# Routed experts on one core: weights split into two fp32r parts or kept whole in fp32, a ring of 9 or 17 weight places, and small experts in two or four column groups

## The chip, the cores and the metric

The kernel runs on one core of one Trainium2 chip. The metric is the time of one execution on the device in microseconds; the median of several runs counts. All rows below come from one execution that the profiler recorded.

## The reference

One block of a hybrid encoder over 1024 tokens of width 1024, all in float32: a state-space mixer and stick-breaking attention, an output projection with a residual, and then a routed mixture of 32 experts, which is the part that the change is about.

```python
h2 = rms_norm(x, g_ffn)                       # g_ffn: one factor per column
gates, expert_id = router(h2)                 # 2 of 32 experts per token
for e in range(32):                           # rows of expert e, in blocks of 128
    y[rows] += gate * ((silu(xb @ w_gate[e]) * (xb @ w_up[e])) @ w_down[e])
x = x + y        # w_gate, w_up: [32, 1024, 512]; w_down: [32, 512, 1024]
```

Each expert has three matrices of 2 MB, 201 MB in all, and each is read once from HBM. With the inputs of the reference its routing gives the 32 experts these numbers of tokens: ten have 32 or fewer (11 to 31), twelve have 33 to 64, six have 65 to 128 (67 to 124), two have 129 to 192 (162, 177) and two have more (198, 219).

## The kernel before

**Stages.** The input projection, the mixer and the attention come first; then the output projection runs over 8 tiles of 128 tokens (`out_open`, `out_part`, `out_close`), with the norm, the store of the normed rows to the DRAM tensor `h2d` (`norm_store`) and the router (`router_turn`, `router_tile`) of each tile. Up to here the order is made by a scheduler. From `moe = tc.manual_schedule(...)` on PE, ACT, DVE and POOL run in the order of the code; only SP's queue, which issues the weight loads, is placed by the scheduler.

**The loop over experts.** Step `e` of the loop computes `in_(e)` (gate and up products), `in_out(e)` (SiLU and product), `prep_x(e + 1)` (the next expert's rows, turned by PE), `down_(e - 1)`, `h_(e)` (the hidden rows turned), and prepares later experts: `prep` makes a one-hot table on DVE, `prep_p` takes row numbers and gates from it on PE, `prep_f` and `prep_g` gather rows of `h2d` by indirect DMAs from POOL, and `down_` ends with an indirect DMA that adds rows to `out` (`scatter`). Experts 0 to 2 come in their own order; the other 29 are sorted by their counts and interleaved (`expert_order`), so that large ones stand among small ones: by counts the order begins 38, 39, 36, 29, 162, 35, 62, 22, 198, 41, 70, 27 and ends 35, 67, 27, 98, 29, 45, 11.

**Sizes.** Expert 0 is always treated as one of over 64 tokens. The count is read into registers of each engine, and branches (`tc.If`) choose the code:

- up to 64 tokens ("few"): the weights are used as they are, in fp32, as the moving operand. The array's 128 columns are two halves of 64: gate goes to PSUM partitions 0 to 63 and up to 64 to 127 (`in_mm_few`), and the two column halves of the down product likewise (`down_mm_few`). 16 matmuls of 512 columns in, 8 down.
- over 64: `w_split` makes of each half matrix a rounded fp32r part `wh` (ACT) and the rest `wl` (DVE), the rows are split too, and each product is three fp32r matmuls (`split_mm`): 48 in, 24 down for a block of 128 tokens. A second block has a second set (`gx`), or the "few" code if it has up to 64 tokens.

**The weight ring.** `units` lists the half matrices, 1 MB each, in the order of use: 4 for `in_`, 2 for `down_`, 192 in all. `load_units` issues them on SP's queue into ring places of 8 KB per partition. There are `RA + RB = 9` places: 5 that are there from the start, and 4 that are made once the tensors of the mixer are given up. A load waits until the unit 9 before it has been used. The first 16 units belong to experts 0 to 2; the later ones need the sorted order, which SP reads from `evi`. The out-projection's weights lie in the `wh` and `wl` buffers (`w_parts`, 8 of each).

Of the kernel before, what the change touches and what calls it, by code (L numbers as in the profile page):

```python
# [18 lines left out]
D = 1024  # L19
# [17 lines left out]
def block_kernel(ctx, tc, x, g_mix, w_in, lam_re, lam_im, log_dt, b_re, b_im, c_re, c_im, d_skip,  # L37
# [11 lines left out]
    mixs = ExitStack()  # L49
    mixp = mixs.enter_context(tc.tile_pool(name="mixp", bufs=1, side="left"))  # L50
# [713 lines left out]
    hlp = ctx.enter_context(tc.tile_pool(name="hlp", bufs=1, side="right", reuse_waits="tile"))  # L764
    HL = 8

    def w_parts():
        return [hlp.tile([P, D], FR, name=nm, bufs=HL) for nm in ("wh", "wl")]

    p3 = o3.enter_context(tc.tile_pool(name="p3", bufs=1, side="right", reuse_waits="tile"))  # L770
# [3 lines left out]
    wo = [w_parts() for _ in range(8)]  # L774
# [3 lines left out]
    gffn_b = p3.tile([P, D], F32, name="gffn_b")  # L778
    nc.scalar.dma_start(gffn_b, dram(g_ffn, 0, [[0, P], [1, D]]))
# [3 lines left out]
    gpc = p3.tile([P, 8], F32, name="gpc")  # L783
# [42 lines left out]
    RA, RB = 5, 4  # L826
    LK = RA + RB
# [7 lines left out]
    rings = {}  # L835
# [12 lines left out]
    def load_units(n):  # L848

        while loaded[0] < min(n, len(units)):  # L850
            k_ = loaded[0]
            ap, s_, rows, hf = units[k_]
            e = s_
            if s_ >= NF:
                if s_ not in ev_sp:
                    ev_sp[s_] = nc.values_load(evs[0][0:1, s_:s_ + 1], engines=[mybir.EngineType.SP],
                                               min_val=0, max_val=NE - 1)
                e = ev_sp[s_]
            pool, nb = (rga, RA) if k_ % LK < RA else (rings["b"], RB)
# [5 lines left out]
    load_units(RA)  # L865


# [39 lines left out]
    slotm = kp.tile([P, P], BF, name="slotm")  # L907
    ts(top, slot, 64.0, 64.0, op0=OP.is_ge, op1=OP.mult)
    tt(slotm, slot, top, op=OP.subtract)
    ts(slot2m, slotm, float(P), None, op0=OP.add)  # L910

    side = kp.tile([P, 1], F32, name="side")
    ts(side, pcol, 64.0, None, op0=OP.is_ge)

# [160 lines left out]
    for i in range(NT):  # L1075
# [11 lines left out]
        if i < NT - 1:  # L1087
            out_close(i)
        if i >= 2:
# [6 lines left out]
    many = kp.tile([P, NE], F32, name="many")  # L1096
    evi = kp.tile([P, NE], I32, name="evi")
    csi = kp.tile([P, NE], I32, name="csi")
    evs.append(evi)
    def expert_order():  # L1100
        tmp = mo.tile([P, 3, NE], F32, name="tmp", tag="gs")
# [11 lines left out]
        ts(many[:, NF:NE], kv, 65.0 * NE, None, op0=OP.is_ge)  # L1113
        ki = mo.tile([P, NS], I32, name="ki")
# [8 lines left out]
    EX = {0: {"in": [], "ins": [], "down": [], "downs": []}}  # L1123
    raw_k, used = [0], [0]

    def early_split(js, eng):
        for j in js:
            raw = raws.pop(raw_k[0])
            raw_k[0] += 1
            parts = [w_parts() for _ in range(2)]  # L1130
            EX[0]["in"].append(raw)
            EX[0]["ins"].append(parts)
            for q_ in range(2):
                r = raw[:, D * q_:D * q_ + D]
                nc.scalar.copy(parts[q_][0], r)
                eng.tensor_tensor(parts[q_][1], r, parts[q_][0].bitcast(F32), op=OP.subtract)
# [7 lines left out]
    early_split(range(1), nc.gpsimd)  # L1144
# [5 lines left out]
    gate_parts(0, NT - 1, nc.gpsimd, nc.scalar.copy)  # L1150
# [4 lines left out]
    tt(away, away, cnt.unsqueeze(1).to_broadcast(sh), op=OP.mult)  # L1155

    tt(posb, own, away, op=OP.add)
# [5 lines left out]
    one_hot(OH, posb[:, :, 0:1], slotb)  # L1163
# [8 lines left out]
    LO, HI, AL = slice(0, HP), slice(HP, P), slice(0, P)  # L1172
# [14 lines left out]
    def x_turn(xg, cg, pt):  # L1187
        for c in range(4):
            nc.tensor.transpose(pt[:, c], xg[:, 4 * cg + c::8], ident)

    def in_mm(blocks, hv):

        for hf in range(2):
            for pa, xh, xl in blocks:
                for k_ in range(4 * hf, 4 * hf + 4):
                    ws = slice(512 * (k_ % 2), 512 * (k_ % 2) + 512)
                    for j in range(2):
                        wh, wl = hv[2 * hf + j][k_ % 4 // 2]
                        split_mm(pa[j], xh[:, k_], xl[:, k_], wh[:, ws], wl[:, ws], k_ == 0, k_ == 7)

    def in_mm_few(pg, xt, hv):
        for k_ in range(8):
            for r, j in ((LO, 0), (HI, 1)):
                w = hv[2 * (k_ // 4) + j]
                mm(pg[r], xt[:, k_], w[:, 512 * (k_ % 4):512 * (k_ % 4) + 512],  # L1205
                   start=k_ == 0, stop=k_ == 7)

    def down_mm(blocks, hv):
        for c in range(4):
            wh, wl = hv[c // 2][c % 2]  # L1210
            for n in range(2):
                ns = slice(512 * n, 512 * n + 512)
                for py, hh, hl in blocks:
                    split_mm(py[n], hh[:, c], hl[:, c], wh[:, ns], wl[:, ns], c == 0, c == 3)

    def down_mm_few(py, ht, hv):
        for c in range(4):
            for n, r in enumerate((LO, HI)):
                w = hv[c // 2]
                mm(py[r], ht[:, c], w[:, D * (c % 2) + 512 * n:D * (c % 2) + 512 * n + 512],  # L1220
                   start=c == 0, stop=c == 3)

# [4 lines left out]
    def prep(e):  # L1227
# [7 lines left out]
        if e:  # L1235
            sl = kp.tile([P, P], BF, name="sl")
            stt(sl, top, many[:, e:e + 1], slotm, op0=OP.mult, op1=OP.add)
# [35 lines left out]
    def prep_it(e):  # L1273
# [9 lines left out]
        with nc.allow_low_precision(reason="whole numbers below 2048"):  # L1283
            nc.vector.tensor_reduce(idx[:, 0:n], d["pi"][:, 0:n, TOK], op=OP.add, axis=AX.X)
            ts(idx[:, 2:2 + n], idx[:, 0:n], 2.0, side, op0=OP.mult, op1=OP.add)
# [14 lines left out]
    def prep_f(e):  # L1300
# [9 lines left out]
        with many_.Else():  # L1310
            gather(d["xg"], d["idx"], LO)
# [20 lines left out]

    def prep_x(e):
# [4 lines left out]
        d["xf"] = xf = mo.tile([P, 8, HP], F32, name="xf", bufs=2)  # L1338
        d["xt"] = xt = mo.tile([P, 8, P], FR, name="xt")
        d["xl"], d["xh2"], d["xl2"] = (mo.tile([P, 8, P], FR, name=nm) for nm in ("xl", "xt2", "xl2"))  # L1340
        xl, xh2, xl2 = d["xl"], d["xh2"], d["xl2"]
        pts = [pb("tr").rearrange("p (c t) -> p c t", c=4) for _ in range(2)]
        pts2 = [pb("gx").rearrange("p (c t) -> p c t", c=4) for _ in range(2)]
        cs = [slice(4 * cg, 4 * cg + 4) for cg in range(2)]
        with tc.If(d["nt"] > P) as two:
            for cg in range(2):
                x_turn(d["xg"], cg, pts[cg])
            for cg in range(2):
                x_turn(xgb, cg, pts2[cg])
        with two.Else():  # L1350
            for cg in range(2):
                x_turn(d["xg"], cg, pts[cg])
        with tc.If(d["na"] > HP) as many_:
            for cg in range(2):
                nc.scalar.copy(xt[:, cs[cg]], pts[cg])
            with tc.If(d["na"] > P):
                with tc.If(d["na"] <= P + HP) as few:
                    nc.scalar.copy(xf[:, cs[0]], pts2[0][:, :, LO])
                with few.Else():
                    for cg in range(2):  # L1360
                        nc.scalar.copy(xh2[:, cs[cg]], pts2[cg])
        with many_.Else():
            nc.scalar.copy(xf[:, cs[0]], pts[0][:, :, LO])
        with tc.If(d["nv"] > HP) as many_:
# [348 lines left out]
```

## Time and profile before

| | |
|---|---|
| time, median of 3 runs | 1335.95 us (1335.26 to 1337.76) |
| the profiled execution: its own time | 1337.16 us |
| its span, first to last instruction | 1335.2 us |
| mean granted clock of TensorE in the span | 0.922 |
| matmul rows in the loop over experts | 606.06 us to 1323.2 us |

The span is what the rows below divide. The execution's own time is 2.0 us longer than its span, and 1.2 us longer than the median of the runs.

### The profile page before, as it was taken

What the parts mean: (1) busy time and instruction counts of PE and PEld (TensorE: products, weight loads), DVE (VectorE), ACT (ScalarE), POOL (GpSimd) and SP (SyncE); (2) the same over time, 40 slices, a digit from 0 to 9 for tenths busy, and PEclk for the clock granted to TensorE, in tenths of its full rate; (3) what the DMA queues carried; (4) which work ended last, traced back from release to release, by engine and by line L of the source; (5) the groups of instructions that cost most, each with busy time, mean ns of one, the idle gap of its engine ahead of it and who ended that gap; (6) DMA issues with size and microseconds to landing.
All of it is one profiled execution on the core that took longest, in us unless ns stands there. A gap on an engine that the chain in (4) does not pass through costs nothing. (4 is left out here: it accounts for less than half of the span.)

```text
span 1335.2 us, 21708 instructions
## 1 busy us (share of the span) xinstructions
PE 1132.6 (85%) x6986; PEld 809.8 (61%) x6986; DVE 773.1 (58%) x1510; ACT 490.3 (37%) x820; POOL 274.3 (21%) x408
## 2 busy tenths in 40 slices
PE   5999999979998899948778989887898688888885
PEld 5999999957766478835335455554456354445541
DVE  6888776797879567778343245553535541445420
ACT  6233534466775532224132133341323420333321
POOL 4141211043345112242111101111101111011101
PEclk9999999979999899977889989988898889889888
DMA  7242321110002343533897968899956989698895
GB/s 249 78 87 53 81 53 53 49 48 1 1 4 82 140 176 127 196 134 114 302 348 270 358 245 337 280 358 382 372 204 243 362 285 354 274 348 290 294 348 174
DMA packets 96744, 272.09 MB, mean 204 GB/s; under 512 B 44324, under 2 KB 57448, under 8 KB 71944
## 3 DMA queue, kind: packets, MB, share of 16 engines
q1 hardware_dynamic: 81528, 238.05, 48.6%
q0 software_dynamic: 12192, 29.93, 9.1%
q8 instruction: 129, 2.11, 0.6%
q10 hardware_dynamic: 2800, 1.22, 0.4%
q14 instruction: 95, 0.78, 0.2%
HBM read 242.56 MB, written 25.43 MB: 201 GB/s over the span
## 5 line engine op out<-in xcount | busy, mean ns | idle before, releaser
L1205 PE MATMUL acc<-raw,xf 128*64 128x512 f32 x672 | 155.4, 610 | 5.5 <-issue 5.5
L1395 DVE TENSOR_TENSOR wl<-raw,wh 128x1024 fp32r<-128x1024 f32 x124 | 143.8, 1219 | 21.6 <-ACT wh L1392 18.0
L92 PE MATMUL acc<-wh,hTh 128*128 128x256 f32 x512 | 146.4, 286 | 4.3 <-ACT wh L88 4.3
L93 PE MATMUL acc<-wl,hTh 128*128 128x256 f32 x512 | 145.1, 283 | 0.0
L94 PE MATMUL acc<-wh,hTl 128*128 128x256 f32 x512 | 144.4, 282 | 0.0
L1392 ACT CAST wh<-raw 128x1024 fp32r<-128x1024 f32 x124 | 121.4, 1048 | 30.2 <-DMA raw<-in_w_down_dram 18.3
L1205 PEld LDWEIGHTS acc<-raw,xf 128*64 128x64 f32 x672 | 51.7, 140 | 93.8 <-issue 90.6
L1429 ACT ACTIVATE hs<-acc 128x512 f32<-128x512 f32 x32 | 19.1, 596 | 231.3 <-PE acc L94 90.8
L1179 POOL DMA_INDIRECT xga<-h2d,idx x32 | 31.3, 978 | 342.0 <-PE y L1220 103.6
L92 PEld LDWEIGHTS acc<-wh,hTh 128*128 128x128 f32 x512 | 97.0, 190 | 4.9 <-ACT wh L88 4.9
L698 DVE TENSOR_TENSOR_SCAN bb<-bb,sb 128x128 f32<-128x128 f32 (+7 forms) x64 | 89.6, 1416 | 13.3 <-POOL bb L695 12.7
L93 PEld LDWEIGHTS acc<-wl,hTh 128*128 128x128 f32 x512 | 96.9, 189 | 0.7 <-DVE wl L89 0.6
L94 PEld LDWEIGHTS acc<-wh,hTl 128*128 128x128 f32 x512 | 96.8, 189 | 0.0
L92 PE MATMUL acc<-wh,xt 128*128 128x512 f32 x176 | 74.8, 425 | 13.7 <-ACT wh L1392 6.4
L695 POOL TENSOR_SCALAR bb<-sb 128x128 f32<-128x128 f32 (+7 forms) x64 | 66.2, 1038 | 94.0 <-ACT sb L694 82.7
L1220 PE MATMUL y<-raw,hf 128*64 128x512 f32 x336 | 82.1, 633 | 3.6 <-DVEq L1500 2.3
L94 PE MATMUL acc<-wh,xl 128*128 128x512 f32 x176 | 73.2, 416 | 0.4 <-DVE xl L1366 0.4
L93 PE MATMUL acc<-wl,xt 128*128 128x512 f32 x176 | 73.0, 415 | 0.0
L1184 POOL DMA_INDIRECT out_dram<-ysa,idx x23 | 38.0, 1653 | 115.3 <-ACTq L1390 37.6
L1433 DVE TENSOR_TENSOR hs<-hs,acc 128x512 f32<-128x512 f32 x11 | 7.6, 687 | 91.5 <-ACT hs L1429 61.4
L92 PE MATMUL y<-wh,ht 128*128 128x512 f32 x88 | 41.8, 475 | 20.9 <-PEq L1482 7.5
L1501 DVE TENSOR_SCALAR ysf<-y,gate 128x512 f32<-128x512 f32 x11 | 8.3, 751 | 83.3 <-PE y L94 65.4
(473 smaller groups left out, 2480.7 us busy)
## 6 DMA issues: line engine op xcount, KB each, us to landing
raw<-in_w_gate_dram SPq DMA_DIRECT2D x64, 1024.0 KB, 13.8
raw<-in_w_up_dram SPq DMA_DIRECT2D x64, 1024.0 KB
raw<-in_w_down_dram SPq DMA_DIRECT2D x64, 1024.0 KB, 14.3
wraw<-in_w_in_dram SPq DMA_DIRECT2D x16, 512.0 KB
wor<-in_w_out_dram SPq DMA_DIRECT2D x8, 512.0 KB, 4.9
xt<-in_x_dram SPq DMA_DIRECT2D x8, 512.0 KB, 7.5
out_dram<-xt SPq DMA_DIRECT2D x8, 512.0 KB, 2.9
h2d<-h SPq DMA_DIRECT2D x8, 512.0 KB, 3.5
```

The lines of the kernel that those rows point to most:

```text
L92: mm(o, ah, bh, start=first, stop=False)
L93: mm(o, ah, bl, start=False, stop=False)
L94: mm(o, al, bh, start=False, stop=last)
L695: nc.gpsimd.tensor_scalar(bt[:, off:T], st[:, off:T], -1.0, 1.0, op0=OP.mult, op1=OP.add)
L698: nc.vector.tensor_tensor_scan(rv, rv, sv, 0.0, op0=OP.mult, op1=OP.add)
L1179: nc.gpsimd.indirect_dma_start(out=dst[r], out_offset=None, in_=h2d, in_offset=bass.IndirectOffsetOnAxis(ap=idx[:n, :1], axis=0))
L1184: nc.gpsimd.indirect_dma_start(out=rows, out_offset=bass.IndirectOffsetOnAxis(ap=idx[:n, :1], axis=0), in_=src[r], in_offset=None, compute ...
L1205: mm(pg[r], xt[:, k_], w[:, 512 * (k_ % 4):512 * (k_ % 4) + 512], start=k_ == 0, stop=k_ == 7)
L1220: mm(py[r], ht[:, c], w[:, D * (c % 2) + 512 * n:D * (c % 2) + 512 * n + 512], start=c == 0, stop=c == 3)
L1392: nc.scalar.copy(w[0], r)
L1395: tt(w[1], r, w[0].bitcast(F32), op=OP.subtract)
L1429: act(hs, pg, AF.Silu)
```

## The change

- Weights are never split. All products with expert weights are fp32 matmuls on the ring places themselves (`in_all`, `in_half`, `in_quarter`, `down_all`, `down_half`, `down_quarter`); `w_split`, `early_split` and `w_parts` go, and with them the parts of the rows (`xl`, `hl`, ...).
- A third size: an expert of up to 32 tokens uses four column groups of 32. `in_quarter` puts gate and up of the first four and of the last four row groups on one group each, so that 4 rounds of 4 matmuls take the place of 8 rounds of 2; a matmul with a table `fold` adds the two partial sums while it turns them. `down_quarter` has 2 rounds of 4. Gathers take 32 rows, and scatters 64 half rows.
- The ring has 17 places: the 5 of before, two in `q_t` and two in `yT` (kept for the whole kernel now), and 8 (`rgw`) where the out-projection's weights lay. 16 units are issued when the out-projection ends, the 17th after `expert_order`.
- `g_ffn` no longer multiplies the stored rows (DVE, or POOL for the last tile); ACT stores them with the norm's factor alone, and DVE applies `g_ffn` when it copies the turned rows out of PSUM (`x_scaled`). The last tile's store goes on ACT's queue.
- In the steps ahead of the loop, the places and gates of all experts are worked out after expert 0's gather has been issued.

```diff
-    RA, RB = 5, 4
-    LK = RA + RB
+    ring = [rga.tile([P, 2048], F32, name=f"rg{j}") for j in range(5)]
+    ring += [q_t.rearrange("p t n -> p (t n)")[:, 2048 * j:2048 * j + 2048] for j in range(2)]
+    ring += [yT.rearrange("p k c t -> p (k c t)")[:, 2048 * j:2048 * j + 2048] for j in range(2)]
+    LK = len(ring) + 8
...
-            t_ = pool.tile([P, 2048], F32, name="raw", tag="raw", bufs=nb)
+            t_ = ring[k_ % LK]
             nc.sync.dma_start(t_.rearrange("p (c n) -> p c n", c=rows), wsrc(ap, e, hf, rows))
...
-        if i == NT - 1:
-            nc.gpsimd.tensor_tensor(h2, d["x2"], gffn_b, op=OP.mult)
-            act(h2, h2, AF.Copy, scale=d["r"])
-        else:
-            stt(h2, d["x2"], d["r"], gffn_b, op0=OP.mult, op1=OP.mult)
-        nc.sync.dma_start(h2d[i * P:(i + 1) * P, :], h2)
+        act(h2, d["x2"], AF.Copy, scale=d["r"])
+        (nc.scalar if i == NT - 1 else nc.sync).dma_start(h2d[i * P:(i + 1) * P, :], h2)
...
-    early_split(range(1), nc.gpsimd)
+    wo_s.close()
+    rgw = ctx.enter_context(tc.tile_pool(name="rgw", bufs=1, side="right", reuse_waits="tile"))
+    ring.extend(rgw.tile([P, 2048], F32, name=f"rw{j}") for j in range(8))
+    load_units(16)
...
+    def x_scaled(xt, cg, pt, r):
+        n = r.stop - r.start
+        cs = slice(4 * cg, 4 * cg + 4)
+        tt(xt[:, cs, r], pt[:, :, r], gpc[:, cs].unsqueeze(2).to_broadcast([P, 4, n]), op=OP.mult)
+
+    def in_all(p, xt, hv):
+        for k_ in range(8):
+            for j in range(2):
+                mm(p[j], xt[:, k_], hv[2 * (k_ // 4) + j][:, 512 * (k_ % 4):512 * (k_ % 4) + 512],
+                   start=k_ == 0, stop=k_ == 7)
...
+    def in_quarter(pg, xt, hv):
+        for k_ in range(4):
+            for u in range(4):
+                mm(pg[32 * u:32 * u + 32], xt[:, 4 * (u // 2) + k_, QU], hv[u][:, 512 * k_:512 * k_ + 512],
+                   start=k_ == 0, stop=k_ == 3)
...
+    def by_count(n, all_, half, quarter):
+        with tc.If(n > HP) as many_:
+            all_()
+        with many_.Else():
+            with tc.If(n > HP // 2) as some_:
+                half()
+            with some_.Else():
+                quarter()
...
         if e:
-            with tc.If(d["nt"] <= HP) as few:
-                in_mm_few(pg, d["xf"], d["in"])
-            with few.Else():
-                in_many()
+            by_count(d["nt"], in_many, lambda: in_half(pg, d["xt"], hv), lambda: in_quarter(pg, d["xt"], hv))
...
     for e in range(NE + 1):
         prep_n(e + 1)
         if e < NE:
             in_(e)
-            used[0] += 4 if e else 0
+            used[0] += 4
             load_units(used[0] + LK)
-        w_split(e - 1, "down", 2)
...
-        w_split(e + 1, "in", 2)
```

How the order moves, at two places. First SP's queue at the end of the output projection (tile 7). `xt` to `out_dram` is the store of a tile's result, `h` to `h2d` that of its normed rows, and `raw`, `yT`, `q_t` and `rw` from `in_w_..._dram` are weight loads. Before:

```order
L861 DMA raw<-in_w_gate_dram 128x2048
L861 DMA raw<-in_w_up_dram 128x2048
L990 DMA out_dram<-xt_6258 128x1024
L861 DMA raw<-in_w_down_dram 128x2048
L1004 DMA h2d<-h_6532 128x1024
L990 DMA out_dram<-xt_6423 128x1024
L1004 DMA h2d<-h_6623 128x1024
L861 DMA raw<-in_w_down_dram 128x2048
```

and now:

```order
L855 DMA yT<-in_w_up_dram 128x2048
L855 DMA yT<-in_w_down_dram 128x2048
L997 DMA out_dram<-xt_6267 128x1024
L1007 DMA h2d<-h_6541 128x1024
L855 DMA rw_6641<-in_w_down_dram 128x2048
L997 DMA out_dram<-xt_6432 128x1024
L855 DMA rw_6642<-in_w_gate_dram 128x2048
L855 DMA rw_6643<-in_w_up_dram 128x2048
L855 DMA rw_6644<-in_w_gate_dram 128x2048
L855 DMA rw_6645<-in_w_up_dram 128x2048
```

Nine units stand ahead of the last tile's stores instead of eight, the seven that follow wait only for the out-projection's last matmuls, and the last store to `h2d` has left this queue.

Second PE's program for the gate and up products of expert 1, from the first branch on it (L1415 before, L1356 now) to the first product behind it. Before:

```order
L1415 COMPARE_AND_BRANCH
L1205 MATMUL acc<-raw,xf 64x512 x16
L1415 UNCONDITIONAL_BRANCH
L1406 COMPARE_AND_BRANCH
L1407 COMPARE_AND_BRANCH
L1205 MATMUL gx<-raw,xf 64x512 x16
L1407 UNCONDITIONAL_BRANCH x2
L1406 UNCONDITIONAL_BRANCH
L1409 COMPARE_AND_BRANCH
L92 MATMUL acc<-wh,xt 128x512
```

and now, from the end of the code for halves on:

```order
L1207 MATMUL acc<-yT,xt 64x512
L1356 UNCONDITIONAL_BRANCH
L1213 MATMUL acc<-rg_5101,xt 32x512
L1213 MATMUL acc<-q_t,xt 32x512 x2
L1213 MATMUL acc<-yT,xt 32x512
L1213 MATMUL acc<-rg_5101,xt 32x512
```

Before, the code for few tokens came first, and behind it stand 16 more fp32 products and 144 fp32r ones that an expert of few tokens jumps over. Now 48 fp32 products for large experts come first, then 16 for halves and 16 for quarters; an fp32 product is two matmuls with a weight load each.

## Rows read from the trace of the kernel before

**Rows 1.** The page: span, TensorE's time, granted clock and DMA share in 40 slices

```profile
span 1335.2 us, 21708 instructions
PE   5999999979998899948778989887898688888885
PEclk9999999979999899977889989988898889889888
DMA  7242321110002343533897968899956989698895
```

**Rows 2.** Busy time by stretch: start and end, length, engines (instructions), clock, DMA

```profile
core 0: us, PE busy (x) PEld busy (x) DVE busy (x) ACT busy (x) POOL busy (x), PEclk, DMA share, GB/s
577.00:606.00 29.00, 7.86 (x103) 6.63 (x101) 24.02 (x67) 10.79 (x17) 15.10 (x23) 0.64 0.26 92
606.00:1323.30 717.30, 597.48 (x2945) 350.57 (x2944) 307.54 (x479) 204.70 (x284) 96.37 (x73) 0.89 0.85 304
```

**Rows 3.** Groups of TensorE's instructions by form: count, busy us, mean ns, idle before

```profile
L1205 PE MATMUL acc<-raw,xf 128*64 128x512 f32 x672 | 155.4, 610 | 5.5 <-issue 5.5
L92 PE MATMUL acc<-wh,xt 128*128 128x512 f32 x176 | 74.8, 425 | 13.7 <-ACT wh L1392 6.4 <-PEq L1407 3.9 <-ACT ysf L1492 1.4
L1205 PE MATMUL gx<-raw,xf 128*64 128x512 f32 x64 | 18.6, 746 | 6.6 <-issue 4.0 <-DVEq L1500 2.6
L92 PE MATMUL gx<-wh,xt 128*128 128x512 f32 x32 | 12.7, 397 | 0.6 <-DVEq L1468 0.6
```

**Rows 4.** Timeline of TensorE in the loop: start, length, what, idle time before

```profile
1079.64 0.39 PE L92 MATMUL acc<-wh,xt 128*128 128x512 f32 x1
...
1081.51 0.39 PE L94 MATMUL acc<-wh,xl 128*128 128x512 f32 x1
...
1083.22 3.65 PE L1220 MATMUL y<-raw,hf 128*64 128x512 f32 x16
...
1087.48 7.09 PE L1205 MATMUL acc<-raw,xf 128*64 128x512 f32 x32
1096.52 0.36 PE L1271 MATMUL y<-ax,OHa 128*128 128x5 bf16 x8 [1.94 <-DVE wl L1395]
...
1102.47 0.80 PE L92 MATMUL y<-wh,ht 128*128 128x512 f32 x1 [3.85 <-PEq L1482]
```

**Rows 5.** Timeline of TensorE in the mixer: whole fp32 products of 128 columns

```profile
204.26 0.39 PE L502 MATMUL m<-TT,U 128*128 128x128 f32 x2
...
205.38 0.39 PE L503 MATMUL m<-CO,HS 128*128 128x128 f32 x2
```

**Rows 6.** Timeline of TensorE: fp32 products on column groups of 32

```profile
448.10 1.05 PE L810 MATMUL acc<-sq,ones 128*32 128x512 f32 x4
```

**Rows 7.** The same, narrower window: one such product alone

```profile
451.13 1.05 PE L810 MATMUL acc<-sq,ones 128*32 128x512 f32 x2 [1.98 <-ACT sq L809]
```

**Rows 8.** TensorE's waits in 606 to 1323.3 us: total, times, longest

```profile
PE y L1271 <- issue: 10.6, 4, 3.7
PE y L1271 <- DVE wl L1395: 10.3, 5, 3.1
PE y L1271 <- DVEq L1436: 9.8, 5, 2.3
PE y L92 <- PEq L1482: 7.5, 3, 3.8
PE y L92 <- ACT wh L1392: 7.3, 2, 4.0
PE acc L92 <- ACT wh L1392: 6.4, 2, 4.0
```

**Rows 9.** DMA queues in 577 to 1323 us: packets, MB, share of 16 engines

```profile
q1 hardware_dynamic: 26640, 192.95, 67.2%
q0 software_dynamic: 8745, 25.42, 14.1%
q8 instruction: 97, 1.59, 0.8%
```

**Rows 10.** SP's queue, 600 to 1336 us: what its weight loads waited for

```profile
SPq L861 <- PE y L93: 142.6, 10, 16.6
SPq L861 <- PE acc L1205: 134.7, 41, 11.3
```

**Rows 11.** Timeline of TensorE: the loop's first product, and its last

```profile
606.06 0.79 PE L92 MATMUL acc<-wh,xt 128*128 128x512 f32 x1
...
1319.56 3.65 PE L1220 MATMUL y<-raw,hf 128*64 128x512 f32 x16 [1.26 <-DVEq L1468]
```

More of the change, by code (lines that the diff above doesn't have):

```diff
@@ L763, in block_kernel @@
     o3 = ExitStack()
[L764 to L770, printed above, removed]
+    wo_s = ExitStack()
+    wop = wo_s.enter_context(tc.tile_pool(name="wop", bufs=1, side="right", reuse_waits="tile"))
+    p3 = o3.enter_context(tc.tile_pool(name="p3", bufs=1, side="left", reuse_waits="tile"))
     h2d = drp.tile([T, D], F32, name="h2d")
@@ L1121, in block_kernel @@
     posb = kp.tile([P, NT, NE], BF, name="posb")
-    EX = {0: {"in": [], "ins": [], "down": [], "downs": []}}
+    EX = {0: {}}
     raw_k, used = [0], [0]
[L1126 to L1136, printed above, removed]
     nc.gpsimd.memset(many[:, 0:1], 1.0)
@@ L1185, in scatter, with x_turn @@
                                      in_=src[r], in_offset=None, compute_op=OP.add)
-    def x_turn(xg, cg, pt):
+    def x_turn(xg, cg, pt, r):
         for c in range(4):
[L1189 to L1199, printed above, removed]
@@ L1209, in down_mm, with down_all @@
+    def down_all(py, ht, hv):
         for c in range(4):
-            wh, wl = hv[c // 2][c % 2]
             for n in range(2):
[L1212 to L1216, printed above, removed]
+                mm(py[n], ht[:, c], hv[c // 2][:, D * (c % 2) + 512 * n:D * (c % 2) + 512 * n + 512],
+                   start=c == 0, stop=c == 3)
@@ L1310, in prep_f @@
         with many_.Else():
-            gather(d["xg"], d["idx"], LO)
+            with tc.If(d["ng"] > HP // 2) as half:
+                gather(d["xg"], d["idx"], LO)
+            with half.Else():
+                gather(d["xg"], d["idx"], QU)
     def prep_g(e):
@@ L1343, in prep_x, with turn, turn2 @@
         pts2 = [pb("gx").rearrange("p (c t) -> p c t", c=4) for _ in range(2)]
-        cs = [slice(4 * cg, 4 * cg + 4) for cg in range(2)]
-        with tc.If(d["nt"] > P) as two:
+        def turn(r):
             for cg in range(2):
-                x_turn(d["xg"], cg, pts[cg])
+                x_turn(d["xg"], cg, pts[cg], r)
+        def turn2(r):
             for cg in range(2):
-                x_turn(xgb, cg, pts2[cg])
-        with two.Else():
+                x_turn(xgb, cg, pts2[cg], r)
@@ L1397, in in_, with next_raws @@
+        by_count(d["nt"], lambda: turn(AL), lambda: turn(LO), lambda: turn(QU))
+        past(d["nt"], lambda: turn2(AL), lambda: turn2(LO))
+        by_count(d["nv"], lambda: scaled(AL), lambda: scaled(LO), lambda: scaled(QU))
+        past(d["nv"], lambda: scaled2(AL), lambda: scaled2(LO))
+    def next_raws(n):
+        raw_k[0] += n
+        return [raws.pop(raw_k[0] - n + j) for j in range(n)]
     def in_(e):
@@ new lines, in h_, with folded @@
+        QT, QB = slice(0, 32), slice(32, 64)
+        def folded():
+            for c in range(4):
+                mm(pt[:, c, LO], d["hs"][:, c::4], fold, start=True, stop=True)
+        with tc.If(d["nt"] > HP // 2) as some_:
+            h_turn(pt, d["hs"])
+            with tc.If(d["nt"] > P):
+                h_turn(pt2, d["hs2"])
+        with some_.Else():
+            folded()
+        by_count(d["na"], lambda: nc.scalar.copy(ht[:, 0:2], pt[:, 0:2]),
+                 lambda: act(ht[:, :, LO], pt[:, :, LO], AF.Silu),
+                 lambda: act(ht[:, :, QT], pt[:, :, QT], AF.Silu))
@@ L1477, in down_ @@
         py2 = [pb("gx"), pb("gx")]
[L1478 to L1488 removed]
+        hv = next_raws(2)
@@ new lines, in v_quarter @@
+        def v_quarter():
+            tt(ys[LO], ys[LO], py[0][LO], op=OP.add)
+            ts(ys[LO], ys[LO], g[LO], None, op0=OP.mult)
+        with tc.If(d["nv"] > HP) as many_:
+            v_many()
+        with many_.Else():
+            with tc.If(d["nv"] <= HP // 2):
+                v_quarter()
+        by_count(d["ng"], lambda: scatter(out_rows, yf, d["idx"], AL),
+                 lambda: scatter(out_halves, ys, d["idxh"], AL),
+                 lambda: scatter(out_halves, ys, d["idxh"], LO))
```

296 lines of the change are left out of this document (118 added, 178 removed).

## The prediction

> **What bounds the kernel now.** I read the page's slices first: TensorE is at 9 tenths up to slice 17, drops to 2 around 590 us, and then stays at 7 to 9 tenths, while the DMA engines, nearly idle before, go to 8 and 9 [rows 1]. The change lies almost wholly in that second part. The busy times by stretch then say how that part divides: from 606 to 1323.3 us TensorE is busy for 597.5 of 717.3 us, DVE for 308, ACT for 205, and the DMA engines for 85% [rows 2]. Two resources are near their end, TensorE and DMA. Which one waits for the other? SP's queue, which issues the weights, waits for TensorE's products: 142.6 us for the down products and 134.7 us for the in products of small experts, to name the two largest [rows 10]. A load waits there for a ring place, and a place comes free when TensorE is done with it. So TensorE is the bound, with 119.8 us of idle time in it (717.3 less 597.5), and DMA is some 15% behind.
>
> That idle time comes in pieces of 2 to 5 us [rows 8, 4]. Some end on the split weights (`wl` 10.3 us, `wh` 7.3 and 6.4). Others end on a branch or on nothing that the profile shows (10.6, 9.8, 7.5), and these stand where TensorE's program jumps: in 1096.52 after a small expert's in product, with 1.94 us, and in 1102.47 ahead of a large one's down product, with 3.85 us [rows 4]. The queue that carries instructions moved 97 packets in the loop [rows 9]; a jump seems to wait for code. [...]
>
> **The change, part by part.**
>
> *Large experts get dearer on TensorE.* One row of 16 split products gives the price of one: eight steps from 1079.64 to 1081.51, 0.234 us each, so 72 of them (48 in, 24 down) are 16.8 us per block of 128 [rows 4]. A whole fp32 product of 512 columns on all 128 columns of the array does not stand in the trace. Two neighbours bound it: 16 products in pairs on two column halves take 7.09 us, 0.886 us a pair [rows 4]; and five whole products of 128 columns take 1.12 us, 0.224 each, which is 0.896 us for 512 columns [rows 5]. They agree, so 24 products cost 21.3 us: +4.5 us per block. Counts follow from the groups: 176/16 = 11 first blocks and 32/16 = 2 second blocks are full, 13 in all [rows 3]. **+58 us.**
>
> *Experts of up to 32 tokens get cheaper.* Today they cost 7.09 + 3.65 us like all small ones [rows 4]; there are 672/32 = 21 of those [rows 3], and by the reference's own routing ten have at most 32 tokens. If four groups run beside each other as two do now, 4 rounds of 0.886 us and 2 more take 5.3 us instead of 10.7; the fold adds about 0.3 (fp32 for a plain turn). 10 x 5.1 = **-51 us.** The bounds are 0 (no better than halves) and -54. That groups of 32 columns do run beside each other is shown for two of them: two products take 1.05 us together [rows 6], and one alone takes the same 1.05 us [rows 7]. I take the full gain.
>
> [...] No run here shows three or four. [...]
>
> The turns of rows before the products keep their number, and half of the eleven middle experts' work does not change at all: halves stay halves. So arithmetic on TensorE is a wash: +58 - 51 = **+7 us.**
>
> *The splits go.* ACT and DVE lose most of their work in the loop. Neither was the bound, so this is worth only the waits: the three split rows of [rows 8] are 24 us, and behind them the queue waits of DVE's and ACT's branches, where a split stood ahead in the queue. What DVE gets in exchange (`x_scaled`, 2 copies with a factor in place of ACT's) and the two extra steps at the end of a quarter (add, scale) stand behind TensorE's down product and turn of the same step; uncovered they would be about 1.4 us a time.
>
> *Code.* A small expert today jumps over 16 fp32 and 144 fp32r products after its own code. Now a half jumps over 48 fp32 products (192 instructions with their weight loads, against 352) and then 16. Shorter jumps, but two per product instead of one, for 21 experts. I take it that a third of these waits goes, with bounds of none and all, and of twice as many.
>
> [...]
>
> Together the idle time goes from 120 to **60 us** (bounds 20 and 130), and with half of its pieces the clock's loss on work from 55 to **35 us** (15 to 60). **-60 - 20 = -80 us.**
>
> *The ring.* 17 places instead of 9 keep the loads going through a large expert. The stream needs, today, 67.2% of 746 us = 501 us for 184 units, 2.72 us each; gathers and scatters 14.1% = 105 us; code 6 us [rows 9]. Ten experts with 32 rows fewer of 4 KB and 64 half rows fewer of 2 KB save 2.6 of 25.4 MB, 11 us. That leaves 601 us, of which 7 units (19 us) go out between 577 and 606 us, a stretch in which the DMA engines are at 26% now [rows 2]. The rest, 582 us, starts once the sorted order is there and expert 0's places come free, at about 615 us: it can't end before 1197 us, and the last down product and scatter (11.9 us today from TensorE's end at 1323.2 [rows 11] to the end of the span) put the floor at about **1210 us**. TensorE's new pace, (717 - 73)/32 = 20.1 us per expert, stands against 582/32 = 18.2 us plus bursts: near enough that the deeper ring is needed but isn't the bound. I add **+4 us** for expert 0 to 2 (its first product is longer at the half clock) and waits for weights at odd places.
>
> *Ahead of the loop.* The norm's multiply leaves DVE for ACT, in a stage where TensorE is at 9 tenths; the last store leaves 2 us earlier, but seven weight units go out beside it and the first gather. I count the start of the loop, 606.06 us [rows 11], as unmoved, within -3 and +6.
>
> *Sum.* Span 1335.2 + 7 - 80 + 4 = 1266 us. The execution's own time is 2 us over its span, and 1.2 us over the median, so the median should be about **1267 us**.
>
> **Rivals.**
>
> - *DMA sets the end.* If nearly all idle time goes (20 us left, clock loss 15), TensorE would be done at 1195 us, and the floor of 1210 us with some unevenness decides: 1210 to 1235 us. For it: 85% DMA share already, with a ring of 9. Against: jumps remain.
> - *Four groups run no faster than two.* Then the 51 us are lost: about 1318 us. For it: only two at a time are in the trace. Against: nothing in [rows 6] and [rows 7] hints at a limit of two.
> - *The idle time stays, and the dearer full blocks decide* (the other side). If the waits belong to jumps and not to splits, and two jumps per product cost as much as one long one, idle and clock loss stay at 175 us and only +7 +4 are left: 1347 us. It decides from the point where less than 11 us of the 175 go. For it: of the six largest rows of [rows 8], 28 us end on branches or on nothing, as much as the 24 on splits. Against: ACT's and DVE's queues will be empty.
> - *It does little*: some 15 us of the 175 go, about 1332 to 1338 us.
>
> **How the numbers follow.** The likeliest case, 1245 to 1290 us around 1267, gets 0.60. DMA as the end gets 0.15, quarters without gain 0.12, the idle time that stays 0.09 and little effect 0.04. A range of 1210 to 1315 us holds the first two and half of the third, some 8 in 10. A measurement of this kernel can tell about 0.2% from no change. Faster by more: 0.60 + 0.15 + 0.12 + 0.01 = 0.88; within: 0.03; slower: 0.09.
>
> **What the profile after would show.** Rows of 16 matmuls (whole) of 0.44 us each, 14.2 us per in product of a full block; quarters at about 3.6 us in and 1.8 us down (7.1 if they run two by two); TensorE's idle time in the loop near 60 us, and what is left of it at jumps, not on ACT or DVE; SP's waits for TensorE shorter, DMA at 0.9 or more; clock above 0.90. I am wrong if quarters take as long as halves, if jumps wait longer than now, or if TensorE waits for weights for tens of microseconds.

## The result: 0.6% slower, and the profile after

The changed kernel takes 1344.45 us (median of 20 runs, 1335.99 to 1350.69), the kernel before, timed beside it, 1335.51 us (20 runs, 1331.6 to 1341.84). The ratio is 1.0063, with a 95% interval of 1.0044 to 1.0081: slower, by little, but clear of the noise. The forecast was 1267 us, and 1344 lies above its whole range of 1210 to 1315. The profiled execution took 1340.88 us, 3.6 us under the median; its span is 1338.9 us and its granted clock 0.932.

Against [rows 1], TensorE, its clock and the DMA engines in the 40 slices of the page:

```profile
PE   5999999969998899948799798788797788887975
PEclk9999999979999999978899899797798898998988
DMA  7332321110001453574898959889956889988781
```

The slice of the turnover (the eighteenth) now has 7 tenths of DMA, where it had 3: the weights do go out ahead of the loop. Behind it nothing looks better. The busy times by stretch say so in numbers, for the two windows of [rows 2] (columns: PE, PEld, DVE, ACT, POOL busy us with instruction counts, clock, DMA share, GB/s):

```profile
577.00:606.00 29.00, 10.59 (x114) 8.72 (x113) 20.53 (x85) 6.71 (x14) 4.93 (x17) 0.66 0.76 295
606.00:1323.30 717.30, 606.32 (x2651) 279.01 (x2652) 172.25 (x450) 50.23 (x106) 85.99 (x69) 0.91 0.81 290
```

In the second window DVE fell from 308 to 172 us and ACT from 205 to 50, as they should. TensorE is busy for 8.8 us more than before, and its idle time is 717.3 - 606.3 = 111.0 us where it was 119.8. Its last product now ends at 1327.6 us instead of 1323.2; to there the idle time is 112 us. The DMA share fell from 0.85 to 0.81. So the idle time, which was to halve, is nearly all still there. Where does it stand now? The waits of TensorE in the loop, to be held against [rows 8]:

```profile
PE acc L1213 <- issue: 35.8, 12, 6.7
PE acc L1207 <- issue: 15.4, 9, 2.5
PE y L1231 <- issue: 9.6, 3, 4.1
PE y L1231 <- PEq L1363: 6.4, 7, 1.1
PE acc L1207 <- DMA rw<-in_w_down_dram: 5.6, 1, 5.6
PE y L1225 <- issue: 5.5, 2, 4.2
PE tr L1449 <- ACTq L1363: 5.3, 5, 1.2
```

No split is left in this list. The waits stand ahead of the in products of quarters (L1213) and halves (L1207) and of the down products of quarters (L1231) and halves (L1225): the codes to which TensorE's program jumps over the full one. "issue" says that the engine waited for nothing that the profile shows. One of these places in the timeline, the longest piece, and a full product for comparison:

```profile
834.32 7.12 PE L1201 MATMUL acc<-yT,xt 128*128 128x512 f32 x16 [1.24 <-issue]
841.28 7.03 PE L1201 MATMUL acc<-rw,xt 128*128 128x512 f32 x16
...
856.41 0.75 PE L1237 MATMUL tr<-ident,hs 128*128 128x128 f32 x4
863.87 6.44 PE L1213 MATMUL acc<-rw,xt 128*32 128x512 f32 x32 [6.71 <-issue]
```

A full in product takes 14.0 us, as forecast (14.2). The quarter's 32 matmuls take 6.4 us, where 3.6 were forecast, behind 6.7 us of nothing. In that gap the queues moved this (window 857 to 863 us; columns: packets, MB, share of the engines):

```profile
q1 hardware_dynamic: 305, 2.22, 92.5%
q0 software_dynamic: 33, 0.06, 5.1%
q8 instruction: 1, 0.02, 1.3%
```

One packet of instructions, amid weights that fill 92.5%. Each of the six other pieces of over 3 us that are put down to "issue" holds one such packet too, and so does the one of 5.6 us that is put down to a load; a piece of 4.0 us ahead of 650.84, in which TensorE waits for DVE, holds none. By itself that proves little: 85 packets in the loop's 721 us are one in 8.5 us, and none lies in the eleven pieces of 1.9 to 2.9 us. More telling is where one of the seven stands, in the middle of a quarter's in product:

```profile
948.01 1.13 PE L1213 MATMUL acc<-q_t,xt 128*32 128x512 f32 x2
953.51 1.07 PE L1213 MATMUL acc<-rg,xt 128*32 128x512 f32 x2 [4.36 <-issue]
```

The matmuls on both sides read the same buffers (`xt` and four ring places), and no branch stands between them. With its operands there and nothing to decide, TensorE stood still for 4.36 us, and one packet of instructions moved meanwhile. And the clock, at another quarter: the idle piece ahead of it, its first 16 matmuls, and the rest (columns as above):

```profile
669.40:671.58 2.18, 0.02 (x1) 0.03 (x1) 0.75 (x2) 0.51 (x2) 1.60 (x1) 0.97 1.01 297
671.58:674.93 3.35, 3.35 (x16) 1.33 (x20) 1.69 (x4) 0.00 (x0) 0.00 (x0) 0.51 1.01 385
674.93:676.80 1.87, 1.87 (x20) 0.58 (x12) 0.00 (x0) 0.00 (x0) 0.00 (x0) 1.00 1.08 333
```

Behind 2.2 us of idle time TensorE has a granted clock of 0.51 of full speed for the first half of the quarter, and of 1.00 for the rest. So the product that pays for the jump also pays for the clock.

### The profile page after: what moved, and what is told of

Read it like the earlier page. It is cut to its first block, busy times and chain, and to the rows that moved or that the text cites. A ratio compares the mean times of both kernels' runs of the same rounds, so it can differ in the third digit from the quotient of the medians.

```text
span 1338.9 us, 20325 instructions
## 1 busy us (share of the span) xinstructions
PE 1146.1 (86%) x6714; PEld 740.1 (55%) x6714; DVE 627.5 (47%) x1490; ACT 338.6 (25%) x646; POOL 252.6 (19%) x399
## 5 line engine op out<-in xcount | busy, mean ns | idle before, releaser
L1437 DVE COPY hs<-acc 128x256 f32<-128x256 f32 x21 | 8.9, 425 | 128.8 <-ACT hs L1431 120.0
L1207 PE MATMUL acc<-rw,xt 128*64 128x512 f32 x192 | 56.8, 706 | 13.6 <-issue 8.0
L1201 PE MATMUL acc<-rg,xt 128*128 128x512 f32 x120 | 56.0, 612 | 3.4 <-issue 2.5
L1201 PE MATMUL acc<-rw,xt 128*128 128x512 f32 x128 | 58.8, 609 | 0.0
L1428 ACT ACTIVATE hs<-acc 128x512 f32<-128x512 f32 x11 | 6.6, 597 | 202.2 <-PEq L1363 85.4
L708 PE MATMUL tr<-ident,bb 128*128 128x128 f32 x288 | 46.4, 286 | 8.1 <-DVE aT L714 3.5
L91 PE MATMUL acc<-wh,mh 128*128 128x512 f32 x128 | 52.2, 410 | 0.0
L721 PE MATMUL acc<-aT,v_t 128*64 128x128 f32 x576 | 46.9, 284 | 5.6 <-DVE aT L714 4.6
L92 PE MATMUL acc<-wl,mh 128*128 128x512 f32 x128 | 50.7, 396 | 0.3 <-DVE wl L796 0.3
L93 PE MATMUL acc<-wh,ml 128*128 128x512 f32 x128 | 50.8, 397 | 0.0
```

The source lines that it names most:

```text
L91: mm(o, ah, bh, start=first, stop=False)
L92: mm(o, ah, bl, start=False, stop=False)
L93: mm(o, al, bh, start=False, stop=last)
L708: nc.tensor.transpose(pt[:, j * P:(j + 1) * P], st[:, off + (j0 + j) * P:off + (j0 + j + 1) * P], ident)
L721: mm(po[64 * r:64 * r + 64, :P], v_t[:, j, 64 * h:64 * h + 64], ATT["T", h, i][:, j, :], start=j == 0, stop=j == i)
L1201: mm(p[j], xt[:, k_], hv[2 * (k_ // 4) + j][:, 512 * (k_ % 4):512 * (k_ % 4) + 512], start=k_ == 0, stop=k_ == 7)
```

## The experiments

**Theory J** (jumps): TensorE's idle pieces stand where its program jumps to code that is not loaded, and the half clock follows them; the change swapped one set of jumps for another. **Rival W**: TensorE waits for weights and gathers, and "issue" hides it. **Rival C**: the half clock has causes of its own. Each run was timed beside the kernel before (1333.5 to 1335.1 us there); ratios are to it, with 95% intervals. For the sizes of code: run e7 adds 31 sets of 16 products and 8 instruction packets of 16.4 KB, so a set of 16 fp32 products with its weight loads is some 4 KB; this is an estimate, and the other sizes of code below follow from it.

**e1: no branches.** The known sizes are written in, on all engines:

```diff
-            d[nm] = nc.values_load(d["ce"], engines=[en], min_val=0, max_val=T + HP)
+        d["nt"] = d["na"] = SIZES[e]       # and d["ng"], d["nv"]
...
-        with tc.If(n > HP) as many_:
+        many_ = n > HP                     # so at every test of the loop
+        for _ in range(many_):
             all_()
```

> The changed kernel with the branches of the loop over experts taken out: which size each expert has is written into the program for these inputs, so TensorE, ACT, DVE and POOL run straight code of the same operations (no register loads of counts). Theory J (TensorE's idle pieces stand where its program jumps to code that is not loaded, and the half clock follows the pieces): some 90 of the 111 us of idle time in the loop and some 40 us of half-clock loss go, 1344 becomes 1210 to 1240 us, where the DMA engines set the end. Rival W (TensorE waits for weights and gathers, the jumps only hide it): 1310 to 1345 us, with the idle pieces put down to DMA instead of issue. Rival C (the half clock has nothing to do with the pieces): idle goes but clock stays near 0.91, about 1250 to 1270 us.

Measured: 1184.69 us (1183.99 to 1186.05), 0.8891 [0.8867, 0.8914]. That is 160 us less than the changed kernel, with the same operations. The window of the loop, the longest waits, and the queues in the loop:

```profile
606.00:1171.80 565.80, 554.54 (x2672) 256.10 (x2670) 169.30 (x451) 51.88 (x107) 87.95 (x70) 0.98 0.98 366
```

```profile
PE gx L1191 <- DMA xgb<-h2d,idx: 4.1, 1, 4.1
PE y L1284 <- DVE ax L1255: 3.3, 1, 3.3
PE y L1284 <- DVE OHb L1162: 1.6, 2, 0.8
```

```profile
q1 hardware_dynamic: 25344, 184.56, 81.4%
q0 software_dynamic: 7580, 22.08, 16.1%
q8 instruction: 21, 0.34, 0.2%
```

Idle time is 11 us, the clock 0.98, no wait on "issue" is left, and 21 instruction packets were fetched where the changed kernel fetched 85. W falls: the same weights come through the same ring, faster. C falls: the half clock went with the pieces. J holds, and more of the time hung on it than I had put there (1210 to 1240 us); the DMA engines, at 98%, are now the bound. This run takes away the tests and the register loads of four engines together with the jumps; that the code itself counts is shown by e5 and e7.

**e2: no branches in the kernel before.** The same edit.

> The kernel before with the branches taken out in the same way, so that the change can be priced without jumps: known_before to known_after. If J holds: of 120 us idle the part on the splits stays (24 us in the three named rows, perhaps 40), 1336 becomes 1245 to 1285 us, and the change without jumps is worth -20 to -50 us. If the jumps cost little in the kernel before: 1320 to 1336 us.

Measured: 1216.73 us (1212.95 to 1218.9), 0.9121 [0.9097, 0.9145]. So the kernel before, too, lost 117 us to its branches, more than the 50 to 90 us that I gave them. Its waits on splits are three rows of 1.0 to 2.4 us now, 4.6 us, where [rows 8] had 24: most of that came with the branches too. Without branches the change is worth 1184.7 against 1216.7, 32 us.

**e3: no quarters.**

```diff
-            with tc.If(n > HP // 2) as some_:
-                half()
-            with some_.Else():
-                quarter()
+            half()
```

> The changed kernel without its third size: experts of up to 32 tokens take the code for 64 (gathers of 64 rows, products in two column halves), so one branch less ahead of each small product and 4 KB less code to jump over. By the working of the prediction (51 us for ten experts) it takes 1395 us. By theory J the quarters run half their time at the half clock behind a jump of 3.1 us on average, and are worth little: 1340 to 1365 us.

Measured: 1314.48 us (1304.53 to 1316.46), 0.9862 [0.9836, 0.9888]: 30 us faster than with quarters, and outside both expectations. The loop of its profiled execution (1304.53 us, the fastest of its runs, 10 us under the median), and its longest waits:

```profile
606.00:1291.70 685.70, 608.70 (x2632) 275.13 (x2630) 164.08 (x430) 52.23 (x107) 88.58 (x70) 0.98 0.86 307
```

```profile
PE acc L1207 <- issue: 32.4, 23, 3.3
PE acc L1201 <- PEq L1446: 10.2, 10, 1.1
PE y L1225 <- PEq L1357: 8.7, 14, 0.8
```

TensorE is busy for as long as with the quarters, 609 us: what quarters save in work, they lose to the clock, 0.91 with them and 0.98 here. And idle time is 77 us in place of 112. One code less ahead of and behind each product is worth more than ten products at half their length.

**e4: small code first.** In each step quarter, half, full in place of full, half, quarter.

```diff
-        with tc.If(n > HP) as many_:
-            all_()
-        with many_.Else():
-            with tc.If(n > HP // 2) as some_:
-                half()
-            with some_.Else():
-                quarter()
+        with tc.If(n <= HP) as few:
+            with tc.If(n <= HP // 2) as least:
+                quarter()
+            with least.Else():
+                half()
+        with few.Else():
+            all_()
```

> The changed kernel with the three codes of each step in the other order, quarter, half, full, by the test for 64 first and then for 32. Theory J: the pieces ahead of quarter products (31 us for ten) go, and pieces of 1 to 2 us come ahead of full products and behind small ones, which jump over the rest, as in the kernel before (26.2 us for 14): 1325 to 1360 us. Rival W: no change, 1344 us, pieces where they were.

Measured: 1334.18 us (1329.37 to 1339.39), 1.0004 [0.9985, 1.0022]: 10 us less than the changed kernel. The pieces moved and did not go: those ahead of the ten quarter products fell from 31.0 to 11.8 us, and those ahead of the eleven full down products rose from 3.6 to 17.9; idle time is 107 us in the loop, where it was 112, and the clock is still at 0.91. Nine of the ten pieces that are left ahead of the quarters are 1.24 to 1.30 us, though no product's code stands between the tests and the quarter. So a part of each piece is the tests and what little else stands ahead of them; for the ten quarters that is 11.8 us of the 31.0.

**e5: less code to jump over.** At 14 of the sorted places there can be no second block, and its code goes:

```diff
+        if not two(e):      # two(e): RANK[e] < 15; the 16th largest of 2048 has at most 128 tokens
+            return
         with tc.If(n > P):
```

> The changed kernel without the code for a second block at the 14 places of the sorted order where no second block can come (the sixteenth largest of 2048 assignments has at most 128 tokens). No operation that runs is taken away, only code that is jumped over: 8 KB of TensorE's in products and 4 KB of its down products at each of these places, and some tests. Theory J by distance: quarter and half products jump 4 to 8 KB instead of 12 to 16, their pieces shrink from 3.1 and 1.7 us to about 1, and some half clock goes with it: 1290 to 1325 us. If only the number of jumps counts: 1335 to 1345 us.

Measured: 1268.36 us (1261.84 to 1270.8), 0.9493 [0.9468, 0.9518]. Nothing that runs was taken away but tests, and 76 us are gone, more than J gave it. Instruction packets 70, idle time 64 us, clock 0.96.

**e6: two codes at each place.** As e5, and full or half at most places, full or quarter at the ten last of the sorted order, small first at the 19 smaller.

```diff
+        few = quarter if RANK[e] >= 19 else half
+        if RANK[e] >= 10:
+            with tc.If(n <= lim(e)) as few_:   # lim: 32 where it is a quarter, else 64
+                few()
+            with few_.Else():
+                all_()
+            return
```

> As the run before, and only two codes at each place: full or half at most places, full or quarter at the ten places of the smallest experts (a larger one there would take the full code), small code first at the 19 places of the smaller experts. So each product has one test, as in the run without quarters, and the ten quarters are kept. J: against the run without quarters (1314 us) the quarters' 51 us less some 12 for the dearer fold come back, and the shorter jumps add 5 to 20 us: 1245 to 1280 us. If the quarter itself costs (and not its branch): 1310 us or more.

Measured: 1224.78 us (1224.09 to 1230.34), 0.9186 [0.9161, 0.921], again more than J gave. The quarter itself doesn't cost; its branch and its code did.

**e7: more code to jump over.**

```diff
+        def in_many_more():
+            in_many()
+            with tc.If(d["nt"] > T):            # never
+                in_all((pg, pu), d["xt"], hv)
```

> The changed kernel with 4 KB more code at the end of the full in product (one more set of 16 products for counts over 1024, which never come): halves and quarters jump 16 and 20 KB instead of 12 and 16, and the eleven full ones take one more jump behind 14 us of products. J by distance: 21 pieces longer by about a quarter, more code blocks loaded, some half clock more: 1350 to 1370 us. If only the number of jumps counts: 1340 to 1348 us.

Measured: 1412.22 us (1410.08 to 1418.77), 1.0579 [1.0552, 1.0605]. 4 KB of code in each step that never runs cost 68 us, more than J's 6 to 26. Its waits:

```profile
PE acc L1213 <- issue: 52.7, 12, 8.0
PE acc L1207 <- issue: 40.0, 11, 7.1
PE y L1231 <- issue: 10.9, 4, 4.4
```

```profile
606.00:1401.20 795.20, 632.19 (x2680) 282.21 (x2680) 173.38 (x452) 50.73 (x107) 87.66 (x71) 0.87 0.75 263
```

The places are those of the changed kernel, the pieces longer (quarters 35.8 to 52.7 us, halves 15.4 to 40.0), and the clock fell to 0.87. They did not all grow by a quarter, as J had it by distance: ahead of or within the in products of halves and quarters the changed kernel has 5 pieces of over 3 us, and e7 has 13 (3.5 to 8.0 us each), while the rest of e7's are 0.9 to 2.9. Only TensorE's program differs here, and 8 more packets (93 instead of 85) moved on queue q8. So q8 carries TensorE's code, and code that never runs made it move 8 packets more.

**e8 and e10: nine ring places**, in e1's kernel.

```diff
-    LK = len(ring) + 8
+    LK = 9
-    load_units(16)        # e10 alone
+    load_units(LK)
```

> The changed kernel without branches (first run), with 9 ring places instead of 17, to price the ring where the DMA engines are at 98%. If the ring carries the loads through large experts as the prediction has it: 10 to 30 us more than 1185, with idle time of TensorE on DMA. If 9 places do: 1183 to 1190 us.

> The changed kernel without branches and with 9 ring places instead of 17, now with 9 loads instead of 16 ahead of the loop (in the eighth run seven loads overwrote weights of the first experts before they were used). If the deeper ring carries the loads through large experts: 1200 to 1225 us, with TensorE waiting for weights of the quarters. If 9 places do: 1183 to 1190 us.

Measured: e8 1219.06 us (1216.51 to 1219.56), but there seven loads overwrote weights of the first experts before they were used, so it computes those experts with other weights. e10 is the clean run: 1218.64 us (1213.3 to 1219.99), 0.9139 [0.9114, 0.9163]. So the ring is worth 34 us (e10 against e1) where nothing else holds TensorE up. The waits of e10 name weights, at the short products of quarters:

```profile
PE acc L1213 <- DMA rg<-in_w_up_dram: 5.7, 3, 3.5
PE acc L1213 <- SPq L1639: 4.7, 3, 1.8
...
PE acc L1213 <- DMA rg<-in_w_gate_dram: 2.3, 2, 1.4
```

Set beside e2 (1216.7 us: splits, 64-column halves and 9 places), it says that with 9 places whole weights and quarters together are worth nothing, within a few us; both kernels have the DMA engines at 96 to 98% there. Without branches the deeper ring makes the whole difference of 32 us; what it would give the kernel with splits was not run.

**e9: less code in the kernel before.** e5's edit there.

```diff
+            self.n, self.k, self.none = n, k, not two(e)   # none: neither the test nor its code
```

> The kernel before, with the code for a second block taken out at the same 14 places as in the fifth run. Theory J: its small products jump over 6 KB of split products instead of 22, and its large ones over less too, so it gains as the changed kernel did (76 us there, with two tests per product; here one): 1265 to 1300 us. If its idle pieces hang on the splits instead: 1320 to 1336 us. Beside the fifth run (1268 us) it gives the worth of the change where less code is jumped over; without any jumps that is 32 us.

Measured: 1274.48 us (1271.38 to 1276.6), 0.9567 [0.9543, 0.9591]. All splits are still there, and 59 us are gone. Beside e5 (1268.4 us, 0.9493) the change is worth some 6 us by the medians and 10 by the ratios.

**e11: full code first at every place**, in e6's kernel (`RANK[e] >= 10` becomes `RANK[e] >= 99`).

> The sixth run (1225 us) with the full code first at every place, so that small products jump over it ahead of themselves (4 KB at 14 places, 12 to 16 KB at the others) instead of behind. If the place of a jump counts (ahead of a product nothing is queued on TensorE; behind it 3.6 to 7 us are): 1235 to 1255 us. If only the distance counts: 1222 to 1230 us.

Measured: 1229.86 us (1223.4 to 1231.5), 0.9226 [0.9199, 0.9253]; e6 has 0.9186 [0.9161, 0.921]. Some 5 us, with intervals that overlap: that the jump stands ahead of a small product or behind it counts little beside how much code lies there.

**e12: still less code**, in e6's kernel.

```diff
+        if full(e):            # RANK[e] < 10: full code without a test
+            return all_()
...
+            if RANK[e] >= 10:  # at most 186 tokens: no second full block
+                return half()
```

> The sixth run (1225 us) with still less code: the ten largest of the sorted order always take the full code without a test (as expert 0 does), and a second full block is only in the code of those ten (the eleventh largest has at most 186 tokens). Nothing that runs is changed. J: five places jump 4 KB less, ten have no test, of the 41 us of idle time some 8 to 15 go: 1205 to 1220 us. If what is left of idle time is not jumps: 1222 to 1230 us.

Measured: 1216.66 us (1212.25 to 1219.55), 0.9136 [0.9113, 0.9159], 8.6% faster than the kernel before. Branches stay where counts decide, so it is a kernel for any inputs; only the places for quarters and for full code without a test were chosen for these.

```profile
606.00:1198.60 592.60, 558.17 (x2667) 264.88 (x2665) 167.93 (x450) 51.64 (x107) 88.56 (x70) 0.98 0.94 351
```

The runs in one table, ordered by the time (without e8, which computes something else). Idle time, pieces, packets and clock are those of each run's profiled execution, which lies within 4.5 us of the median, but 10 us under it in e3. Idle time is the loop's window, to the end of TensorE's last product, less its busy time; long pieces are those of 2 us or more in the timeline, added up; packets are those of the larger instruction queue (q8) in the loop.

| kernel | median us | packets | idle us | in long pieces | clock |
|---|---|---|---|---|---|
| e7 dead code | 1412.2 | 93 | 163 | 110 | 0.87 |
| changed | 1344.5 | 85 | 112 | 62 | 0.91 |
| before | 1335.5 | 96 | 120 | 84 | 0.89 |
| e4 small first | 1334.2 | 84 | 107 | 55 | 0.91 |
| e3 no quarters | 1314.5 | 67 | 77 | 16 | 0.98 |
| e9 before, less code | 1274.5 | 69 | 79 | 46 | 0.94 |
| e5 less code | 1268.4 | 70 | 64 | 22 | 0.96 |
| e11 two codes, full first | 1229.9 | 53 | 43 | 11 | 0.97 |
| e6 two codes | 1224.8 | 53 | 41 | 11 | 0.98 |
| e10 no branches, 9 places | 1218.6 | 21 | 30 | 11 | 0.97 |
| e2 before, no branches | 1216.7 | 23 | 39 | 24 | 0.97 |
| e12 two codes, less | 1216.7 | 46 | 34 | 9 | 0.98 |
| e1 no branches | 1184.7 | 21 | 11 | 7 | 0.98 |

Among the kernels with the changed kernel's products and ring (all but e3, e10 and the three of before), packets, idle time and time fall together. Theory J had the direction right in every run that tests it, and the size too small in e1, e2, e3, e5, e6 and e7: it says what the time hangs on, not how much.

## Why the prediction was wrong

**Code is the step that failed.** The prediction said of the jumps: "Shorter jumps, but two per product instead of one, for 21 experts. I take it that a third of these waits goes", and made of it, with the splits, idle time from 120 to 60 us and the clock's loss from 55 to 35. Measured: idle time 120 to 112; the clock from 0.89 to 0.91. No run shows the 55 us for the clock, nor the 35. What the traces show in their place: the granted clock before was 0.50 from 606 to 610 us and 1.00 from 1079.64 to 1083.22 us, and over the loop's 717 us it was 0.11 short of full speed before and is 0.09 short now, which is 79 us and 65 us of the window. TensorE is busy for 0.83 and 0.85 of it, so by my estimate some 12 of these 14 us fall on work. Of the 80 us some 20 came, 8 of idle time and 12 of the clock. With that and the 39 us of the quarters (below) the sum reads +58 - 39 - 20 = -1 us; the loop of the profiled execution became 4 us longer, which is as near as a clock of two digits allows. Two things were wrong in it. The jumps are much more of the idle time than I took: without branches 11 us of 112 are left in the changed kernel (e1), 39 of 120 in the one before (e2). And shorter jumps by products passed are not fewer waits: the change put a third code into every in and down product and so left 85 of 96 instruction packets to fetch. The third rival, which got 0.09, gave 1347 us, and its mechanism is what the runs show: two jumps per product cost about as much as one long one. That its number is so near is partly luck. It wanted less than 11 of the 175 us to go, and some 20 went; the quarters gave 12 us less than it had, which made up for that.

What the traces show of the fetching of code: the packets are 1.39 MB / 85 = 16.4 KB each, one lies in each piece of over 3 us that is put down to "issue" in the changed kernel, and e7's 8 more packets came with code that never runs. No run here shows in what order code is fetched, how much of it TensorE holds loaded, nor what the pieces of 1 to 3 us are made of beyond the tests.

**Splits.** "the three split rows of [rows 8] are 24 us". They went, but in e2 they are 4.6 us with all splits in place, and e9 gains 59 us without touching one. So they hung on the branches and not on the work of splitting. On whose branches is not shown: in five of the pieces that the trace before puts down to splits (2.8 to 4.1 us, ending at 872.08, 1005.22, 1049.36, 1055.79 and 1067.96 us) one packet moved on q8, so a part may be TensorE's own jumps.

**Large experts dearer, +58.** Right: 14.0 us per full in product, from the two rows at 834 and 841 us.

**Quarters, -51.** The mechanism was right, and a part of the size off. Four groups do run side by side: in e1 ten quarter in products take 36.4 us in all, 3.64 each, and a down product 1.92 (from the first matmul's start to the last one's end in the timeline). The 32 matmuls of a full in product, which run one after the other, take 14.0 us, and the 32 of a quarter 3.64, which is 3.85 times as fast. The fold cost more than the 0.3 us of the forecast: 80 matmuls of 20.7 us in the group below are 2.07 us for each of ten, a plain turn is 0.75 (the row at 856 us), so 1.3. That makes some 39 us at full clock. In the changed kernel itself, however, the mean of a quarter's matmul is 770 ns, and 595 in e1, where no jump stands ahead of it (the same group of both kernels, and the fold):

```profile
L1213 PE MATMUL acc<-rw,xt 128*32 128x512 f32 x144 | 35.5, 770 | 12.6 <-issue 12.6
L1449 PE MATMUL tr<-fold,hs 128*128 128x64 f32 x80 | 20.7, 401 | 6.2 <-ACTq L1363 5.3 <-PE y L1225 0.9
```

```profile
L1213 PE MATMUL acc<-rw,xt 128*32 128x512 f32 x144 | 25.4, 595 | 0.0
```

The ten in products took 51.6 us there, not 36. With the idle pieces (31 us ahead of them, 14 ahead of their down products) the size that was to save 51 us lost 30 (e3).

**The ring, +4 and "isn't the bound".** In the changed kernel nothing contradicts it: one wait of 5.6 us names a load. Its own worth shows only where the jumps are gone, 34 us (e10 against e1).

**DMA's floor, 1210.** Too high: e1 takes 1184.7 us. By its queue row a 1 MB unit took 81.4% of 565.8 us / 176 = 2.62 us, not the 2.72 that I worked out from [rows 9]. The DMA share of 0.9 or more, which I expected of the profile after, shows only as the jumps go: 0.81 in the changed kernel, 0.94 in e12, 0.98 in e1.

**Ahead of the loop.** Right: the first product starts at 606.3 us, 606.06 before.

**Slips that change nothing in the sum.** The piece of 1.94 us at 1096.52, which the prediction takes for a branch's, is put down to DVE's `wl` in [rows 4]. The page's slice around 590 us shows 4 tenths for TensorE [rows 1], not 2; 577 to 606 us alone has 0.27 [rows 2].

## What to carry to other kernels

Where an engine's program branches over unrolled code, count the code and not only the branches: a wait that the profile puts down to "issue", or to the engine's own queue, near a branch can be a fetch of code. Here one packet of instructions moved in each of the changed kernel's seven pieces of over 3 us on "issue", and one in the 3.85 us that the kernel before put down to TensorE's own queue ahead of 1102.47 us [rows 4]; 4 KB more of code in each step, by the estimate above, cost 68 us (e7). Before adding a special case that saves a few us of work, price the code that all other cases must now pass; and take away code that a bound on the data rules out (the 16th largest of 2048 has at most 128), which gave 76 us here for a few lines. To learn how much of the time hangs on branches, write the known sizes in and time that; to learn how much of it is code, add code that never runs.

## What the runs showed that I had not expected

- Code that never runs is dear out of proportion: 4 KB more per step (e7) made the pieces ahead of quarters 17 us and those ahead of halves 25 us longer and cost 68 us; taking 12 KB and more away at 14 places (e5) gave 76. What grows is the number of pieces of over 3 us, 5 to 13, more than their length. Why 4 KB makes so many more stays open; no run varied the distance in finer steps.
- The short products pay twice: at 671.58 us a quarter's first half ran at a granted clock of 0.51, behind 2.2 us of idle time. Over the table's runs the clock of the loop falls as the long pieces add up: 0.97 or 0.98 with 7 to 16 us of them, 0.91 with 55 and 62, 0.87 with 110.
- Four column groups of 32 get through 32 matmuls 3.85 times as fast as a full product does one after the other (3.64 us against 14.0).
